# A decoder layer on one core: the first two token blocks are multiplied for v before their norm

## The chip, the cores and the metric

The kernel runs on one core of one Trainium2 chip. The metric is the device time of one execution in microseconds (us), lower is better. The core has five engines with a queue of instructions each: PE (matrix products; loads of the stationary operand are shown as PEld), DVE (elementwise work), ACT (activation functions and copies), POOL (small helpers) and SP (which issues most of the transfers). Each engine works through its own queue in the order in which the instructions stand there, and waits by semaphores for the others.

## The reference, cut to what matters

```python
def layer(x, norm1_g, w_in, ...):                   # x: 512 tokens x 1024 channels
    u = x * rsqrt(mean(x * x, -1) + EPS) * norm1_g  # RMSNorm, one factor for each token
    a_glu, q, k, v, r, g_low, gate_a, gate_b = split(u @ w_in)
    ...                                             # conv branch, gated attention, merge, FFN
```

The change lies in the first few products: `v[:, 0:512] = u @ w_in[:, v columns 0:512]`. It rests on the factor of the norm being one number for each token: `((x * g) @ w) * r` is the same as `(x * g * r) @ w`.

## The kernel before

**Products.** All large products are made of float32 operands split into two parts, a high one in a rounded format (`hi`, made by a copy on ACT) and the remainder (`lo`, made by a subtraction on DVE). A product is three matmuls: low times high, high times low, high times high (`mm3`, L283 to L285). A weight block of 128 x 1024 arrives in a `raw` buffer (three of them) by a DMA that SP issues (L166), and `split_weight` makes `whi` (ACT, L238) and `wlo` (DVE, L241) of it; there are four buffers for each. A list `order` names all weight blocks in the order of use, and `weight()` keeps the splitting two blocks ahead (`LOOK`).

**The first stage.** x is handled in four blocks of 128 tokens (t = 0 to 3). `norm1(t)` squares and sums the block on ACT (L398, with a read of the accumulator), adds EPS on DVE (L400), takes the power -1/2 on POOL (L331) and scales the block on DVE by the factor and the gains (L404, two halves). The gains were spread over all partitions by two matmuls with a row of ones (L389). `to_channels(t)` then turns the block: for each of two groups of four channel tiles, four transposes on PE (L360), a copy to the high part `uh` on ACT (L364) and the subtraction for the low part `ul` on DVE (L365). `u1` holds the result for all later products with `w_in`.

**The products for v.** `values(0, next_tokens)` runs `row_half` with the tokens outside: the four weight blocks of `w_v` are all split first, and then each token block t goes through its eight channel tiles (24 matmuls of 128 x 512) into one PSUM bank. In the middle of a token block (`MID` = 4 tiles) `next_tokens(t)` issues the transposes of block t+1 and `norm1(t+2)`. `v_done` copies each bank out (L428). When the last block is under way, `prefetch` splits the first blocks of the next stage, `w_glu`.

**What sets the order.** Everything up to there stands inside `tc.manual_schedule(engines=START)`: PE, ACT, DVE and SP get their instructions in the order in which the program text issues them. What comes after it (the `w_glu` products, `col_tile`, with the conv taps as filler on DVE) is placed by the planner.

## Time and profile before

| | us |
|---|---|
| median of 3 runs | 855.03 |
| lowest, highest | 854.35, 855.71 |
| the profiled execution's own time | 854.89 |
| its span in the profile | 853.0 |
| PE busy, PEld busy | 839.1, 693.6 |
| DVE busy, ACT busy, POOL busy | 642.9, 373.1, 19.5 |

The profile covers one execution; starts are counted from the start of its span. Rows of instructions read: start, duration, engine, line, operation, output <- inputs, shape, count, and in brackets the idle time of the engine before it with what ended it.

### The profile page before, as it was taken

How to read it: one execution, taken by the hardware profiler on the slowest of the kernel's cores; microseconds unless marked ns; L12 is line 12 of the kernel's file. 1: busy time of each engine (PE TensorE's matmuls, PEld its weight loads, DVE VectorE, ACT ScalarE, POOL GpSimd, SP SyncE). 2: the span in 40 equal slices, each digit the busy share in tenths (PEclk: the TensorE clock that was granted, in tenths of full speed). 3: DMA queues.
4: the chain of work that ended last, by engine and by line, in shares of the span. 5: the costliest groups of instructions: out<-in, count | busy, mean ns of one | idle time of the engine just before them, and what ended most of it. 6: DMA issues, size and time to landing. Idle time of an engine off the chain costs nothing.

```text
span 853.0 us, 9893 instructions
## 1 busy us (share of the span) xinstructions
PE 839.1 (98%) x3838; PEld 693.6 (81%) x3838; DVE 642.9 (75%) x895; ACT 373.1 (44%) x515; POOL 19.5 (2%) x36
## 2 busy tenths in 40 slices
PE   8999999999999999999999999999999999999995
PEld 5888888888888888788888898888888888888884
DVE  5479879999998788744553458779857779857797
ACT  5523337435533522359322336444344445344444
POOL 1000000000100100000000000000000000000001
PEclk9999999999999999999999999999999999999999
DMA  7233232323222332322332163332542222533213
GB/s 274 91 107 107 91 101 88 100 74 99 75 78 80 127 99 99 99 74 90 109 124 102 59 222 124 100 99 75 196 149 98 95 80 75 192 129 100 75 38 111
DMA packets 26848, 91.74 MB, mean 108 GB/s; under 512 B 3041, under 2 KB 3169, under 8 KB 26802
## 3 DMA queue, kind: packets, MB, share of 16 engines
q1 hardware_dynamic: 26802, 91.11, 32.2%
q8 instruction: 30, 0.49, 0.2%
q14 instruction: 16, 0.13, 0.0%
HBM read 89.01 MB, written 2.10 MB: 107 GB/s over the span
## 4 chain that ended last, share of the span: by engine, by line
PE 96%; DVE 2%; DMA 1%; POOL 0%; ACT 0%; issue 0%; SPq 0%; POOLq 0%; DVEq 0%
PE mm L283 30%; PE mm L285 30%; PE mm L284 30%; PE ax L689 1%; DMA raw<-in_w_v_dram 1%; PE ax L360 1%; PE ax L691 1%; PE ax L671 1%; PE ax L283 1%; PE ax L284 1%; PE ax L285 1%; PE ax L658 0%; PE ax L706 0%; PE ax L657 0%; DVE hres L919 0%; DVE wlo L224 0%
## 5 line engine op out<-in xcount | busy, mean ns | idle before, releaser
L283 PE MATMUL mm<-uh,wlo 128*128 128x512 f32 (+1 forms) x768 | 294.8, 384 | 0.0
L285 PE MATMUL mm<-uh,whi 128*128 128x512 f32 (+1 forms) x768 | 292.4, 381 | 0.0
L284 PE MATMUL mm<-ul,whi 128*128 128x512 f32 (+1 forms) x768 | 292.0, 380 | 0.0
L238 ACT CAST whi<-raw 128x1024 fp32r<-128x1024 f32 x124 | 129.5, 1045 | 165.6 <-PE mm L285 134.8
L241 DVE TENSOR_TENSOR wlo<-raw,whi 128x1024 fp32r<-128x1024 f32 x124 | 151.0, 1220 | 52.5 <-ACT whi L238 52.1
L285 PEld LDWEIGHTS mm<-uh,whi 128*128 128x128 f32 x768 | 144.4, 188 | 27.9
L284 PEld LDWEIGHTS mm<-ul,whi 128*128 128x128 f32 x768 | 144.5, 188 | 27.2
L283 PEld LDWEIGHTS mm<-uh,wlo 128*128 128x128 f32 x768 | 144.5, 188 | 27.2
L448 DVE SCALAR_TENSOR_TENSOR c<-h,pp,c 128x511 f32<-128x511 f32 (+14 forms) x240 | 162.6, 732 | 0.7
L828 DVE SCALAR_TENSOR_TENSOR tmp<-mm,pp,tmp 128x511 f32<-128x511 f32 x88 | 65.7, 748 | 60.0 <-ACT tmp L826 58.8
L826 ACT ACTIVATE tmp<-mm,pp 128x512 f32<-128x512 f32 x44 | 34.3, 780 | 70.3 <-PE mm L285 70.3
L223 ACT CAST whi<-kept 128x1024 fp32r<-128x1024 f32 (+1 forms) x24 | 23.3, 975 | 20.7 <-PE mm L285 8.8
L331 POOL TENSOR_TENSOR rstd<-var,mhalf 128x1 f32<-128x1 f32 (+1 forms) x20 | 15.4, 778 | 690.1 <-DVE var L788 473.6
L224 DVE TENSOR_TENSOR wlo<-kept,whi 128x1024 fp32r<-128x1024 f32 (+1 forms) x24 | 26.9, 1129 | 0.5 <-ACT whi L223 0.5
L223 ACT CAST whi<-raw 128x1024 fp32r<-128x1024 f32 (+1 forms) x18 | 17.5, 977 | 21.7 <-PE mm L285 13.8
L283 PE MATMUL mm<-whi,ul 128*128 128x512 f32 x64 | 25.3, 396 | 1.2 <-DVE ul L365 1.2
L285 PE MATMUL mm<-whi,sh 128*128 128x512 f32 x66 | 26.1, 395 | 0.0
L284 PE MATMUL mm<-wlo,sh 128*128 128x512 f32 x66 | 26.1, 395 | 0.0
L283 PE MATMUL mm<-whi,sl 128*128 128x512 f32 x66 | 26.0, 394 | 0.0
L283 PE MATMUL mm<-h,wlo 128*128 128x512 f32 x64 | 25.7, 402 | 0.0
L283 PE MATMUL mm<-whi,h 128*128 128x512 f32 x64 | 25.4, 397 | 0.0
L285 PE MATMUL mm<-h,whi 128*128 128x512 f32 x64 | 25.3, 395 | 0.0
(198 smaller groups left out, 1114.5 us busy)
## 6 DMA issues: line engine op xcount, KB each, us to landing
raw<-in_w_up_dram SPq DMA_DIRECT2D x44, 512.0 KB, 3.4
raw<-in_w_down_dram SPq DMA_DIRECT2D x20, 512.0 KB, 3.4
raw<-in_w_glu_dram SPq DMA_DIRECT2D x16, 512.0 KB, 3.3
kept<-in_w_down_dram SPq DMA_DIRECT2D x10, 512.0 KB, 4.7
raw<-in_w_v_dram SPq DMA_DIRECT2D x8, 512.0 KB, 3.7
raw<-in_w_qk_dram SPq DMA_DIRECT2D x8, 512.0 KB, 3.3
raw<-in_w_r_dram SPq DMA_DIRECT2D x8, 512.0 KB, 3.3
raw<-in_w_gb_dram SPq DMA_DIRECT2D x8, 512.0 KB, 3.3
```

Source lines behind the costliest of these rows:

```text
L223: nc.scalar.copy(hi, raw)
L224: nc.vector.tensor_tensor(lo, raw, hi.bitcast(F32), ALU.subtract)
L238: nc.scalar.copy(hi, raw)
L241: pace[0] = nc.vector.tensor_tensor(lo, raw, hi.bitcast(F32), ALU.subtract)
L283: nc.tensor.matmul(acc, ll, rh, start=first, stop=False, **kw)
L284: nc.tensor.matmul(acc, lh, rl, start=False, stop=False, **kw)
L285: nc.tensor.matmul(acc, lh, rh, start=False, stop=last, **kw)
L331: nc.gpsimd.tensor_tensor(r, v, mhalf[:, :n], ALU.pow)
L360: nc.tensor.transpose(tr[:, k * P : (k + 1) * P], un[:, c : c + P], ident)
L448: nc.vector.scalar_tensor_tensor(y[:, s:], c[:, : T - s], w, y[:, s:], ALU.mult, ALU.add)
L826: nc.scalar.activation(z, acc, AF.Identity, bias=pp[:, PP_FB + m : PP_FB + m + 1], scale=w[2])
L828: nc.vector.scalar_tensor_tensor(z[:, s:], acc[:, : T - s], w[j], z[:, s:], ALU.mult, ALU.add)
```

## The change

Token blocks 0 and 1 (`EARLY` = 2) are no longer normed ahead of the products for the first half of v. Their transposes are multiplied by the gains only (one number for each partition after the transpose; the gains arrive as eight rows by a DMA that ACT issues, and one transpose turns them), split into temporary high and low parts (`eu`), and multiplied with the weights one weight block at a time, both token blocks together (`by_parts`: within a call first all high x high, then weight low x high, then weight high x low). `v_done` scales their banks by the norm's factor `rs[t]`. Their normed form, which all later products need in `u1`, is made later by `normalize(t)`, in the middle of token blocks 2 and 3: a matmul spreads the factors over the partitions, DVE multiplies, ACT makes the high part and DVE the low part. Blocks 2 and 3 (`late_acts`) are scaled ahead of the transpose; the gains are multiplied in behind it. The first two weight blocks are split in halves. `warm(n)` issues n matmuls of ones on PE: 13 at the start, 4 behind the first transposes and one between each two of the first six products; `WARM[2]` and `WARM[3]` are not used. x block 1 is loaded ahead of the second weight block, x block 2 ahead of the constants `pp`. The rest of the program, from the `w_glu` products on, is as before, and stands in the same order on every engine.

```diff
-WARM = 3
+WARM = (13, 4, 2, 3)
 MID = 4
+EARLY = 2
...
             lo = wp.tile([P, D], F32R, tag="wlo", name=nm("wlo"), bufs=4)
+            if halves:
...
+                cols = [slice(j * T, (j + 1) * T) for j in range(2)]
+                for c in cols:
+                    nc.scalar.copy(hi[:, c], raw[:, c])
+                return [lambda c=c: low(c) for c in cols]
...
+    nc.scalar.dma_start(rows8, a["norm1_g"].rearrange("(k p) -> k p", p=P))
     load_x(0)
-    load()
     load()
     load_x(1)
     load()
-    gain1 = [mm_bank(), mm_bank()]
-    for j in range(2):
-        nc.tensor.matmul(gain1[j], ones[0:1, :], row[:, j * T : (j + 1) * T], start=True, stop=True)
...
+    load()
+    load_x(2)
+    warm(WARM[0])
+    nc.tensor.transpose(idle[:, P : P + KT], rows8, ident[0:KT, 0:KT])
+    nc.vector.tensor_copy(gains, idle[:, P : P + KT])
...
+    def with_gain(tr, g):
+        f = heap()
+        by_channel = gains[:, g * 4 : g * 4 + 4].unsqueeze(2).to_broadcast([P, 4, P])
+        nc.vector.tensor_tensor(by_four(f), by_four(tr), by_channel, ALU.mult)
+        return f
...
+    def normalize(t):
+        r = ax_bank()
+        nc.tensor.matmul(r[:, :P], rs[t].to_broadcast([P, P]), ident, start=True, stop=True)
+        for g in range(2):
+            f = by_four(xg[t, g])
+            nc.vector.tensor_tensor(f, f, r[:, :P].unsqueeze(1).to_broadcast([P, 4, P]), ALU.mult)
+            hi, lo = in_u1(t, g)
+            high(hi, f)
+            low(lo, f, hi)
+
+    def late_acts(t):
+        nc.vector.tensor_scalar(xs[t], xs[t], rs[t], None, ALU.mult)
+        for g in range(2):
+            f = by_four(with_gain(transposed(xs[t], g), g))
+            hi, lo = in_u1(t, g)
+            high(hi, f)
+            low(lo, f, hi)
...
-        nc.scalar.copy(vt[t, n], acc)
+        if n == 0 and t < EARLY:
+            nc.scalar.activation(vt[t, n], acc, AF.Copy, scale=rs[t])
+        else:
+            nc.scalar.copy(vt[t, n], acc)
...
-    values(0, next_tokens)
+    early_acts(0, 0)
+    early_high(0, 0)
+    early_acts(0, 1)
+    warm(WARM[1])
+    lows = split_weight(True)
+    lows[0]()
+    early_low(0, 0)
+    lows[1]()
+    load()
+    early_high(0, 1)
+    early_low(0, 1)
+    accs = [mm_bank() for _ in range(EARLY)]
+    by_parts(accs[0], 0, (0, 1), lambda: warm(1))
+    squares(0)
+    early_acts(1, 0)
+    early_high(1, 0)
+    early_low(1, 0)
+    early_acts(1, 1)
+    by_parts(accs[1], 1, (0, 1))
+    for part in split_weight(True):
+        part()
+    load_x(3)
+    load()
+    early_high(1, 1)
+    early_low(1, 1)
+    squares(1)
+    for t in range(EARLY):
+        by_parts(accs[t], t, (2, 3))
+    split_weight()
+    for t in range(EARLY):
+        by_parts(accs[t], t, (4, 5))
+    squares(2)
+    late_acts(2)
+    split_weight()
+    for t in range(EARLY):
+        by_parts(accs[t], t, (6, 7))
+        v_done(t, 0, accs[t])
+    for t in range(EARLY, NT):
+        acc = mm_bank()
+        by_parts(acc, t, range(4))
+        if t == EARLY:
+            squares(3)
+            late_acts(3)
+        normalize(t - EARLY)
+        by_parts(acc, t, range(4, KT))
+        if t == NT - 1:
+            prefetch(LOOK)
+        v_done(t, 0, acc)
```

More of the change, by code (lines that the diff above doesn't have):

```diff
@@ L211, in sum_down, with split_weight @@
         return raw
-    def split_weight(between=None):
+    def split_weight(halves=False, between=None):
         if len(ready) < len(order):
@@ L237, in split_weight, with low @@
             lo = wp.tile([P, D], F32R, tag="wlo", name=nm("wlo"), bufs=4)
+            if halves:
+                ready.append((hi, lo))
+                def low(c):
+                    nc.vector.tensor_tensor(lo[:, c], raw[:, c], hi[:, c].bitcast(F32), ALU.subtract)
+                cols = [slice(j * T, (j + 1) * T) for j in range(2)]
+                for c in cols:
+                    nc.scalar.copy(hi[:, c], raw[:, c])
+                return [lambda c=c: low(c) for c in cols]
             nc.scalar.copy(hi, raw)
-            if between:
-                between()
             pace[0] = nc.vector.tensor_tensor(lo, raw, hi.bitcast(F32), ALU.subtract)
@@ L368, in trunk_layer @@
     u1 = new_acts()
-    row = tp.tile([P, D], F32, tag="gain", name=nm("row"), bufs=1)[0:1, :]
+    acts1 = by_k(u1)
     nc.vector.memset(ones, 1.0)
     nc.gpsimd.memset(mhalf, -0.5)
-    xs = {}
+    xs, rs, xg, eu = {}, {}, {}, {}
     def load_x(t):
@@ L376, in load_x, with by_four @@
         nc.sync.dma_start(xs[t], a["x"][t * P : (t + 1) * P, :])
+    def by_four(t):
+        return t.rearrange("p (k t) -> p k t", k=4)
     start = tc.manual_schedule(engines=START)
     start.__enter__()
-    nc.sync.dma_start(row, a["norm1_g"].unsqueeze(0))
+    rows8 = tp.tile([P, P], F32, tag="gain", name=nm("gains"), bufs=1)[0:KT, :]
+    nc.scalar.dma_start(rows8, a["norm1_g"].rearrange("(k p) -> k p", p=P))
     load_x(0)
-    load()
     load()
@@ L385, in trunk_layer, with warm @@
     load()
-    gain1 = [mm_bank(), mm_bank()]
-    for j in range(2):
-        nc.tensor.matmul(gain1[j], ones[0:1, :], row[:, j * T : (j + 1) * T], start=True, stop=True)
-    warm = ax_bank()
-    for _ in range(WARM):
-        nc.tensor.matmul(warm[:, :P], ident, ident, start=True, stop=True)
-    def norm1(t):
-        xt = xs[t]
+    load()
+    load_x(2)
+    idle = ax_bank()
+    def warm(n):
+        for _ in range(n):
+            nc.tensor.matmul(idle[:, :P], ones, ones, start=True, stop=True)
@@ new lines, in trunk_layer, with transposed @@
+    gains = cp.tile([P, KT], F32, name="gains")
+    warm(WARM[0])
+    nc.tensor.transpose(idle[:, P : P + KT], rows8, ident[0:KT, 0:KT])
+    nc.vector.tensor_copy(gains, idle[:, P : P + KT])
+    def transposed(x, g):
+        tr = ax_bank()
+        for k in range(4):
+            c = (g * 4 + k) * P
+            nc.tensor.transpose(tr[:, k * P : (k + 1) * P], x[:, c : c + P], ident)
+        return tr
+    def with_gain(tr, g):
[3 more added lines that the diff above has]
+        return f
@@ L397, in norm1, with in_u1, high, low @@
+    def in_u1(t, g):
+        return [x[:, :, t * P : (t + 1) * P] for x in u1[g]]
+    def high(hi, f):
+        nc.scalar.copy(hi, f)
+    def low(lo, f, hi):
+        nc.vector.tensor_tensor(lo, f, hi.bitcast(F32), ALU.subtract)
+    def squares(t):
         ss = small(1, "ss")
-        nc.scalar.activation(junk(D), xt, AF.Square, scale=1.0 / 32.0, accum_out=ss)
+        nc.scalar.activation(junk(D), xs[t], AF.Square, scale=1.0 / 32.0, accum_out=ss)
         v = small(1, "var")
         nc.vector.tensor_scalar(v, ss, EPS, None, ALU.add)
-        r = rsqrt(v, 1)
@@ L402, in norm1 @@
-        for j in range(2):
-            s = slice(j * T, (j + 1) * T)
-            nc.vector.scalar_tensor_tensor(xt[:, s], xt[:, s], r, gain1[j], ALU.mult, ALU.mult)
-    norm1(0)
-    split_weight()
-    split_weight(lambda: to_channels(xs[0], u1, 0, (0,)))
-    to_channels(xs[0], u1, 0, (1,))
-    load_x(2)
-    norm1(1)
-    split_weight()
-    split_weight()
-    load_x(3)
-    acts1 = by_k(u1)
-    def next_tokens(t):
-        if t + 1 < NT:
-            to_channels(xs[t + 1], u1, t + 1)
-        if t + 2 < NT:
-            norm1(t + 2)
+        rs[t] = tp.tile([P, 1], F32, tag="r1", name=nm("r1"), bufs=NT)
@@ new lines, in squares, with early_acts, early_high, early_low @@
+        nc.gpsimd.tensor_tensor(rs[t], v, mhalf[:, :1], ALU.pow)
+    def early_acts(t, g):
+        xg[t, g] = with_gain(transposed(xs[t], g), g)
+        eu[t, g] = [by_four(heap(F32R)) for _ in range(2)]
+    def early_high(t, g):
+        high(eu[t, g][0], by_four(xg[t, g]))
+    def early_low(t, g):
+        low(eu[t, g][1], by_four(xg[t, g]), eu[t, g][0])
+    def normalize(t):
[7 more added lines that the diff above has]
+            low(lo, f, hi)
@@ L427, in v_done, with by_parts @@
         vt[t, n] = heap()
-        nc.scalar.copy(vt[t, n], acc)
-    def values(n, middle):
-        row_half("w_v", n * KT // 2, n, acts1, KT, v_done, n == 1, middle)
-    values(0, next_tokens)
+        if n == 0 and t < EARLY:
+            nc.scalar.activation(vt[t, n], acc, AF.Copy, scale=rs[t])
+        else:
+            nc.scalar.copy(vt[t, n], acc)
+    ws = [order[j] for j in range(KT // 2)]
+    assert ws == [("w_v", j) for j in range(KT // 2)]
+    used[0] = len(ws)
+    def by_parts(acc, t, ks, between=None):
+        for i, (wi, ai) in enumerate(((0, 0), (1, 0), (0, 1))):
+            for k in ks:
+                act = eu[t, k // 4][ai][:, k % 4, :] if t < EARLY else acts1[k][ai][:, t * P : (t + 1) * P]
+                j = slice((k % 2) * T, (k % 2 + 1) * T)
+                first, last = k == 0 and i == 0, k == KT - 1 and i == 2
+                nc.tensor.matmul(acc, act, ready[k // 2][wi][:, j], start=first, stop=last)
+                if between:
+                    between()
+    early_acts(0, 0)
[46 more added lines that the diff above has]
+        v_done(t, 0, acc)
     start.__exit__(None, None, None)
@@ L581, in gate @@
                 nc.vector.tensor_tensor(ls[h], ls[h], ab[h], ALU.subtract)
-    values(1, gate)
+    row_half("w_v", KT // 2, 1, acts1, KT, v_done, True, gate)
     def gl(n, tag, bufs):
```

## The prediction, made before the changed kernel ran

> **What bounds the kernel now.** I read the page first, then the waits of PE, then the timeline of the first 40 us.

> ```profile
> span 853.0 us, 9893 instructions
> PE 839.1 (98%) x3838; PEld 693.6 (81%) x3838; DVE 642.9 (75%) x895; ACT 373.1 (44%) x515; POOL 19.5 (2%) x36
> ...
> PE mm L389 <- DMA row<-in_norm_g_dram: 2.4, 1, 2.4
> PE mm L283 <- DVE ul L365: 1.2, 1, 1.2
> PE mm L283 <- DVE hres L919: 0.8, 1, 0.8
> ```

> The reader is to see that PE is the bound: the third-longest wait of PE in 853 us is already 0.8 us, so what delays PE in the first stage delays the end one for one, and what lets it start sooner can be won. The timeline shows how the first stage runs (start, duration, engine, line).

> ```profile
> 0.90 0.17 DVE L370 MEMSET ones<- 128x128 f32 x1 [0.90 <-PEq L1063]
> 2.45 3.75 PE L389 MATMUL mm<-row,ones 1*128 1x512 f32 x4 [2.45 <-DMA row<-in_norm_g_dram]
> 4.52 1.06 ACT L398 ACTIVATE junk<-x 128x1024 bf16<-128x1024 f32 x1 [2.44 <-DMA x<-in_x_dram]
> 6.12 1.65 PE L393 MATMUL ax<-ident 128*128 128x128 f32 x6
> 7.57 1.82 PE L360 MATMUL ax<-ident,x 128*128 128x128 f32 x8
> 10.62 0.50 PE L283 MATMUL mm<-whi,ul 128*128 128x512 f32 x1 [1.24 <-DVE ul L365]
> ...
> 20.11 0.39 PE L285 MATMUL mm<-whi,uh 128*128 128x512 f32 x1
> 20.79 0.40 PE L285 MATMUL mm<-whi,uh 128*128 128x512 f32 x1
> 21.02 1.04 PE L360 MATMUL ax<-ident,x 128*128 128x128 f32 x8
> 36.47 0.39 PE L283 MATMUL mm<-uh,wlo 128*128 128x512 f32 x1
> ```

> The first product for v starts at 10.62, the first of `w_glu` at 36.47. A warm product takes 0.227 us of PE (three in 20.79 - 20.11 = 0.68). Eight transposes take 1.04 us warm and 1.82 cold: 0.11 and 0.21 each. Between 10.62 and 36.47 lie 25.85 us: 96 products (21.8) and 24 transposes (2.7), with 1.4 us of waits. The change rebuilds only this stretch; from the first product of `w_glu` on the order is the old one. So the sum is the new start of that product against 36.47, added to the profiled execution's own 854.89 us (the median of the runs, 855.03, is 0.14 more).

> **The prices.** Groups of the first 40 us, then of the whole run, then single rows of the timeline and of the chain.

> ```profile
> L241 DVE TENSOR_TENSOR wlo<-raw,whi 128x1024 fp32r<-128x1024 f32 x8 | 9.7, 1221 | 5.7 <-ACT whi L238 5.4
> L238 ACT CAST whi<-raw 128x1024 fp32r<-128x1024 f32 x8 | 8.4, 1050 | 4.6 <-DMA raw<-in_w_v_dram 2.2 <-PE mm L285 1.4 <-DMA raw<-in_w_glu_dram 1.0
> L404 DVE SCALAR_TENSOR_TENSOR x<-x,rstd,mm 128x512 f32<-128x512 f32 x8 | 5.6, 745 | 2.8 <-POOL rstd L331 2.8
> L365 DVE TENSOR_TENSOR ul<-ax,uh 128x512 fp32r<-128x512 f32 x8 | 5.2, 686 | 4.7 <-ACT uh L364 4.7
> L398 ACT ACTIVATE junk<-x 128x1024 bf16<-128x1024 f32 x4 | 4.2, 1060 | 4.0 <-DMA x<-in_x_dram 4.0
> L428 ACT COPY h<-mm 128x512 f32<-128x512 f32 x4 | 2.4, 589 | 3.3 <-PE mm L285 3.3
> L331 POOL TENSOR_TENSOR rstd<-var,mhalf 128x1 f32<-128x1 f32 x4 | 2.2, 554 | 19.8 <-DVE var L400 19.8
> L398 ACT ACTIVATION_READ_ACCUMULATOR junk<-x 128x1 f32 x4 | 0.8, 190 | 0.0
> L400 DVE TENSOR_SCALAR var<-ss 128x1 f32<-128x1 f32 x4 | 0.6, 152 | 5.7 <-ACT junk L398 5.5
> ...
> L525 ACT CAST h<-h 128x512 fp32r<-128x512 f32 x8 | 5.0, 625 | 3.0 <-DVE h L771 3.0
> ...
> 32.59 1.05 ACT L238 CAST whi<-raw 128x1024 fp32r<-128x1024 f32 x1 [0.77 <-PE mm L285]
> 33.68 3.94 DVE L241 TENSOR_TENSOR wlo<-raw,whi 128x1024 fp32r<-128x1024 f32 x3 [3.74 <-ACT whi L238]
> 842.84 0.49 DVE L892 TENSOR_SCALAR hres<-hres,rstd 128x512 f32<-128x512 f32 x1 [0.44 <-POOL rstd L331]
> 844.33 1.19 DVE hres L919 x2
> ```

> A pass of DVE over 128x512 takes 0.69 until the next engine may go on, and 0.60 until DVE's next one (two in 1.19). ACT's copy to the high part takes 0.62 from SBUF. A hand-over from engine to engine is 0.04 (33.68 after 32.59 + 1.05).

> **What decides: pairs in turn.** The new forms of the activations cost DVE two passes for each group of four channel tiles, where it had one besides the norm: `with_gain` or the multiplication in `normalize` makes f, ACT makes the high part of f, DVE the low part. On DVE's queue the order is f, low, f, low: low waits for ACT, and the next f stands behind low. So a group costs 0.69 + 0.04 + 0.62 + 0.04 + 0.60 = 2.0 us in turn, of which DVE works 1.3. Blocks 2, 3, 0 and 1 have two groups each: 16 us of such pairs, in a stage in which PE has 12 us of products for blocks 2 and 3.

> **The start of the products.** Removed are the gain matmuls, the wait for their row, and the chain squares, EPS, POOL, scaling ahead of the first transposes. x block 0 is issued first (it was second), so it lands some 0.4 us before 4.5. But 13 warm-up matmuls now stand ahead of its transposes: as L393 shows, one float32 matmul is two records (six for `WARM` = 3), so they are 26, and from 1.1 us (ones set at 0.90 + 0.17) at 0.21 each they last to 6.7. The trace has one case of PE's speeding up: eight slow transposes up to 9.39, fast products from 10.62, so 7 to 8 us after its first work at 2.45. With the same here it comes at 8 or 9, and all 26 are slow. Then: transposes of the first group 6.9 to 7.9, f 8.6, high part 9.25, half of the first weight block on ACT 9.8. First product at 9.8, 0.8 sooner than before. If PE speeds up after 3.5 us, it is 8.4.

> **To the second weight block.** Six products with six warm-ups between them (0.22 each, fast by then) and 0.6 of waits for the halves of `wlo` end at 13.1; block 1's transposes, f and high part come in turn (0.44 + 0.2 + 0.69 + 0.62 + hand-overs), and token block 1's products start at 15.2 after 1.1 of waiting. ACT meanwhile has in its queue: the high part, two halves of the second weight block, the other high part, squares(1) with its read (1.06 + 0.19), and only then the third weight block: 18.2 to 19.2, its `wlo` 20.5. PE's 12 products with it end at 22.8.

> **The first new stall.** Behind them stand the transposes of block 2 on PE, and on ACT both its high parts ahead of the fourth weight block's. The chain is one transposed group (0.6), f, high, low, f, high (0.69 + 0.62 + 0.60 + 0.69 + 0.53), `whi` (1.05) and six hand-overs: 5.0 us, of which PE works 0.9 on transposes. It stands for 4.1 us, and after two products for 0.8 more, until `wlo` of that block is there (1.22 behind `whi`). It goes on at 27.8, and blocks 0 and 1 are done at 31.35.

> **The second new stall.** ACT now copies out the two banks, 0.59 each, and only then squares block 3, though that has long landed: copy 0.6, squares 1.25, EPS 0.15, POOL 0.55, scaling by one number over 128x1024, transposes 0.6. No row has that scaling; it lies between 0.49 (L892, half the size) and 1.22 (a two-operand pass of that size), I take 0.8, near the first, of the same operation. With hand-overs the first f of block 3 starts at 35.65. From there six pairs (block 3, then `normalize(0)` and `normalize(1)`) at 2.0 are 12.0, and behind them stand the first blocks of `w_glu` on the same two queues: `whi` 1.05 and `wlo` 1.22, of which 0.6 lies beside the last low part. That is 49.2. PE from 31.35 has 48 products (10.9), eight transposes (0.9), two small matmuls (0.4) and 0.9 of waiting for block 3: done at 44.5, and waits 4.8 us for `wlo`, which its first `w_glu` product reads.

> **The sum.** 49.2 - 36.47 = 12.7 us. As a check by terms: start 0.8 sooner; warm-ups between products and factor matmuls +1.8; early waits +2.5; stalls 4.1 + 0.8 + 0.9 + 4.8 = 10.6; the old waits of 1.4 gone: 12.7. So 854.89 + 12.7 = 867.6.

> **What costs nothing.**

> ```profile
> raw<-in_w_v_dram SPq DMA_DIRECT2D x8, 512.0 KB, 3.7
> x<-in_x_dram SPq DMA_DIRECT2D x4, 512.0 KB, 5.3
> ```

> On SP the fourth weight block waits until `wlo`'s second half of the first is made (11.7) and lands 3.7 later, 15.4; ACT takes it at 26.7. Block 3 of x is behind it and lands by 17.5 to 21, needed at 32. The `w_glu` blocks follow by 22, needed at 46. Should these covers go, each would only lengthen a chain that is later anyway. The gains' DMA on ACT stands before any work of ACT. POOL's four powers wait in turn as before. The scale in `v_done` rides on a copy that was there.

> **Bounds.** The clock's start: 47.8 to 49.3. The passes with gains at 0.745 (as L404) for 0.69, eight of them in the chains: +0.5. The scaling: -0.3 to +0.4. Hand-overs of 0.06 for 0.04: +0.5. So 866 to 869 for this case.

> [...]

> ```profile
> 844.35 0.40 PE L285 MATMUL mm<-whi,ah 128*128 128x512 f32 x1
> ...
> 844.80:848.80 4.00, 0.00 (x0) 0.00 (x0) 2.83 (x8) 2.44 (x6) 1.42 (x2) 1.00 0.56 207
> 848.90:853.00 4.10, 0.00 (x0) 0.00 (x0) 0.11 (x1) 0.35 (x1) 0.00 (x0) 0.50 0.68 251
> ```

> At the end PE idles from 844.75, and the granted clock (third column from the right) is 1.00 for four more microseconds, then 0.50. So an idle stretch of about 4 us can halve it, and both stalls are that long. If it happens, products take about twice as long (as the transposes did at the start, 0.21 for 0.11) until PE has been busy again for a while, 7 to 8 us there as an upper end; with 3 to 6 us that is 1.5 to 3 us for each stall, 869 to 873. [...] The trace agrees with a delay of about 4 us.

> **The rivals.** (a) The forecast: 867.6, chance 0.64. (b) Forecast plus the halved clock: about 870. The stalls are just at the length that the one case of the trace shows: chance 0.18. (c) The pairs overlap on DVE: a group then costs DVE's own work, 1.3 for 2.0. The second chain shortens by 4.2 us, the first by at most 0.7: about 863. Against it stands the order of the queue; for it, that DVE is free a third of the time. Chance 0.11. (d) The other side: PE bounds the stage, since all pairs hide. Then the early start counts: 9.8 + 26.2 of PE work = 36.0, or 34.6 with the early clock: 853.0 to 854.4. This decides once the second chain fits PE's 12.2 us: 4.3 + 6p + 1.6 below 12.2, p below 1.05; DVE's own two passes are 1.3, so only a chain that starts sooner as well would do. Chance 0.04. Another 0.03 goes to what I have not thought of. That the change should not do what it says I see no way for: the four queues are written out in program order.

> **How the numbers follow.** A measurement of this kernel can tell about 0.2% (1.7 us) from no change. Faster by more: half of (d) and a little, 0.03; within: the other half, 0.02; slower: 0.95. The range leaves out the ends of (b) and (c): 862.5 to 872.

> **What would show it.** Right: in the profile after, PE's longest waits are of about 4 us for `whi` or `wlo` in the first 50 us, DVE's rows alternate f and low with ACT's copy between, and the first `w_glu` product starts near 49. Wrong: f of the next group starts before low of this one; or that product starts before 40 us.

## The result, and the profile after

| | before | after |
|---|---|---|
| median of the runs (us) | 854.7 (854.35 to 855.71, 4 runs) | 866.67 (866.02 to 867.43, 4 runs) |
| profiled execution (us) | 854.89 | 866.07 |
| its span (us) | 853.0 | 864.0 |
| first product for `w_glu` starts (us) | 36.47 | 51.22 |

The ratio after to before is 1.0137, with an interval of 1.0123 to 1.0151: the change costs 1.4%. The forecast was 867.6, in a range of 862.5 to 872.0. The span and the row of busy times of the page after:

```profile
span 864.0 us, 9987 instructions
PE 842.2 (97%) x3879; PEld 701.3 (81%) x3879; DVE 648.9 (75%) x908; ACT 375.2 (43%) x521; POOL 19.5 (2%) x36
```

PE's busy time rose by 3.1 us, the span by 11.0: most of the loss is idle time of PE. The waits of PE (line, what it waits for: us in total, times, longest) say where:

```profile
PE mm L293 <- DVE wlo L251: 4.4, 1, 4.4
PE mm L496 <- ACT whi L250: 3.9, 1, 3.9
PE ax L408 <- DVE ones L382: 1.1, 1, 1.1
PE mm L496 <- ACT h L433: 1.0, 1, 1.0
```

The first two rows are waits that before did not have. The timeline of after (start, duration, engine, line) shows both with what goes on beside them:

```profile
1.11 5.76 PE L408 MATMUL ax<-ones 128*128 128x128 f32 x26 [1.11 <-DVE ones L382]
9.57 0.50 PE L496 MATMUL mm<-whi,h 128*128 128x512 f32 x1 [0.62 <-ACT whi L248]
22.65 1.04 PE L420 MATMUL ax<-ident,x 128*128 128x128 f32 x8
27.60 1.22 PE L496 MATMUL mm<-whi,h 128*128 128x512 f32 x2 [3.92 <-ACT whi L250]
33.59 0.69 ACT L481 ACTIVATE h<-mm,r 128x512 f32<-128x512 f32 x1 [1.87 <-PE mm L496]
36.17 0.75 DVE L468 TENSOR_SCALAR x<-x,r 128x1024 f32<-128x1024 f32 x1 [0.66 <-POOL r L444]
37.73 0.69 DVE L426 TENSOR_TENSOR h<-ax,gains 128x512 f32<-128x512 f32 x1 [0.81 <-PE ax L420]
45.65 0.68 DVE L462 TENSOR_TENSOR h<-h,ax 128x512 f32<-128x512 f32 x1
46.37 0.62 ACT L433 CAST uh<-h 128x512 fp32r<-128x512 f32 x1 [0.87 <-DVE h L462]
47.02 0.69 DVE L436 TENSOR_TENSOR ul<-h,uh 128x512 fp32r<-128x512 f32 x1 [0.69 <-ACT uh L433]
47.63 0.68 DVE L462 TENSOR_TENSOR h<-h,ax 128x512 f32<-128x512 f32 x1
48.34 0.62 ACT L433 CAST uh<-h 128x512 fp32r<-128x512 f32 x1 [1.36 <-DVE h L462]
49.94 2.36 DVE L251 TENSOR_TENSOR wlo<-raw,whi 128x1024 fp32r<-128x1024 f32 x2 [0.25 <-ACT whi L250]
51.22 0.80 PE L293 MATMUL mm<-uh,wlo 128*128 128x512 f32 x1 [4.41 <-DVE wlo L251]
```

Read DVE from 45.65 on: f (L462), then ACT's high part (L433), then the low part (L436), and only then the next f, 1.98 us after the last one. The `w_glu` weights (L251) stand behind all of them, and PE stands still for 4.41 us.

What the waits alone don't show is in the windows of after (stretch, length, busy time and count of PE, PEld, DVE, ACT, POOL, then the granted clock, DMA share, GB/s):

```profile
23.70:27.00 3.30, 0.00 (x0) 0.00 (x0) 1.93 (x4) 1.63 (x3) 0.00 (x0) 1.00 0.00 1
27.10:33.80 6.70, 6.16 (x14) 4.42 (x15) 1.45 (x2) 1.34 (x3) 0.00 (x0) 0.50 0.26 78
33.90:46.80 12.90, 12.32 (x60) 9.74 (x58) 6.76 (x11) 4.82 (x9) 0.55 (x1) 1.00 0.00 0
46.90:50.90 4.00, 0.00 (x0) 0.00 (x0) 2.94 (x4) 2.64 (x5) 0.00 (x0) 1.00 0.00 0
51.00:54.30 3.30, 3.08 (x7) 2.51 (x8) 2.53 (x3) 1.28 (x2) 0.00 (x0) 0.50 0.60 187
54.40:58.00 3.60, 3.60 (x17) 2.99 (x16) 1.23 (x1) 2.33 (x2) 0.00 (x0) 1.00 0.94 270
```

Behind each stall the granted clock is 0.50: for 6.8 us behind the first, for 3.4 behind the second. From start to start a product takes 0.43 us there (behind the second stall they start at 51.81, 52.24 and 52.67), about twice the 0.227 of full pace.

The third part of the account lies far from the change. A product deep in the kernel can be followed by its own start: the shift, its start after minus its start before, is 14.75 us at the first `w_glu` product, 16.31 seven products later, 16.07 at 292 us, and from there it falls, in stretches and without a jump, to 13.5 at 494, 11.7 at 753, 11.2 at 841. PE has no wait in that stretch, in either kernel. Windows from one product to the same product, 480.95 to 741.05 of before and 494.46 to 752.78 of after:

```profile
480.95:741.05 260.10, 260.10 (x1246) 218.24 (x1245) 198.93 (x256) 116.46 (x147) 1.66 (x3) 1.00 0.36 118
...
494.46:752.78 258.32, 258.31 (x1246) 218.00 (x1245) 198.10 (x255) 116.51 (x147) 1.65 (x3) 1.00 0.35 119
```

The same 1246 products, PE busy throughout, the clock full in both, and 1.78 us less. So the account of the 11.0 us is: stage up to `w_glu` +14.75, half clock behind it +1.56, quicker products later -5.1, the last few us -0.2.

### The profile page after: what moved, and what is told of

Same layout as the page of the kernel before. It is cut to its first block, busy times and chain, and to the rows that moved or that the text cites. A ratio compares the mean times of both kernels' runs of the same rounds, so it can differ in the third digit from the quotient of the medians.

```text
span 864.0 us, 9987 instructions
## 1 busy us (share of the span) xinstructions
PE 842.2 (97%) x3879; PEld 701.3 (81%) x3879; DVE 648.9 (75%) x908; ACT 375.2 (43%) x521; POOL 19.5 (2%) x36
## 4 chain that ended last, share of the span: by engine, by line
PE 94%; DVE 3%; ACT 1%; issue 0%; POOL 0%; POOLq 0%; ACTq 0%
PE mm L293 29%; PE mm L295 28%; PE mm L294 28%; PE mm L496 1%; PE ax L803 1%; PE ax L408 1%; PE ax L785 1%; PE ax L805 1%; PE ax L293 1%; PE ax L294 1%; PE ax L295 1%; DVE h L426 1%; ACT uh L433 1%; DVE ul L436 0%; PE ax L370 0%; PE ax L772 0%
## 5 line engine op out<-in xcount | busy, mean ns | idle before, releaser
L250 ACT CAST whi<-raw 128x1024 fp32r<-128x1024 f32 x122 | 127.3, 1045 | 160.3 <-PE mm L295 128.2
L251 DVE TENSOR_TENSOR wlo<-raw,whi 128x1024 fp32r<-128x1024 f32 x122 | 148.6, 1220 | 48.4 <-ACT whi L250 48.4
L341 POOL TENSOR_TENSOR rstd<-var,mhalf 128x2 f32<-128x2 f32 (+1 forms) x16 | 13.3, 837 | 666.3 <-DVE var L902 469.9
L225 ACT CAST whi<-raw 128x1024 fp32r<-128x1024 f32 (+1 forms) x18 | 17.5, 978 | 21.9 <-PE mm L295 13.2
L293 PE MATMUL mm<-ch,wlo 128*128 128x512 f32 x64 | 25.1, 393 | 0.0
L295 PE MATMUL mm<-ch,whi 128*128 128x512 f32 x64 | 25.0, 391 | 0.0
## 6 DMA issues: line engine op xcount, KB each, us to landing
raw<-in_w_up_dram SPq DMA_DIRECT2D x44, 512.0 KB, 3.4
raw<-in_w_down_dram SPq DMA_DIRECT2D x20, 512.0 KB, 3.4
raw<-in_w_glu_dram SPq DMA_DIRECT2D x16, 512.0 KB, 3.4
kept<-in_w_down_dram SPq DMA_DIRECT2D x10, 512.0 KB, 4.3
raw<-in_w_v_dram SPq DMA_DIRECT2D x8, 512.0 KB, 3.5
raw<-in_w_qk_dram SPq DMA_DIRECT2D x8, 512.0 KB, 3.3
raw<-in_w_r_dram SPq DMA_DIRECT2D x8, 512.0 KB, 3.4
raw<-in_w_gb_dram SPq DMA_DIRECT2D x8, 512.0 KB, 3.3
```

Source lines behind the costliest of these rows:

```text
L225: nc.scalar.copy(hi, raw)
L250: nc.scalar.copy(hi, raw)
L251: pace[0] = nc.vector.tensor_tensor(lo, raw, hi.bitcast(F32), ALU.subtract)
L293: nc.tensor.matmul(acc, ll, rh, start=first, stop=False, **kw)
L295: nc.tensor.matmul(acc, lh, rh, start=False, stop=last, **kw)
L341: nc.gpsimd.tensor_tensor(r, v, mhalf[:, :n], ALU.pow)
```

## The experiments

After this result the theory had two parts. **Theory P**: pairs in turn make the two stalls, and the stalls bring the half clock, at about 2.0 us before `w_glu` and 1.6 after. **Theory A**: the quicker products have nothing to do with the order of the work. The change adds a 32-byte tile (`gains`) and a set of small ones (`r1`) ahead of tiles allocated later. How far that moves them is the author's reckoning from the order and the sizes of the tiles in the two programs; no trace shows an address, and all offsets below are of this reckoning. By it weights and `uh`/`ul` move by 32 bytes per partition, and the heap, the convolution's and the FFN's tiles (the heap family below) by 160; modulo 256 bytes the two families (weights, then heap) stood at 64 and 192 before, and stand at 96 and 96 after; `gains` moves both families alike, and it is the set `r1`, allocated between them, that changes the distance of the heap from the weights, from 128 to 0. The rival to A was that the later start itself, against DMA and the other engines, makes the products quicker.

### Before, with the later tiles moved by 128 bytes

An unused tile is all that is added; the heap family then stands at 64, as the weights do.

```
     ps = pool("psum", 1, bass.MemoryType.PSUM)
+    pool("pad", 1).tile([P, 32], F32, name="pad")
     heap_scope, hp = scoped("heap", 26)
```

> The kernel before with one change: an unused tile of 128 bytes per partition in front of the heap, so that the heap, the conv and the FFN tiles lie 128 bytes higher. Nothing else moves. Theory A (addresses): a product whose operands come from the heap or the FFN tiles takes 0.232 us before and 0.227 after because these tiles lie at another offset modulo 256 bytes than the weight buffers (192 against 64 before, 96 and 96 after); with the pad they lie at 64 and 64, so some 1,000 products win 0.005 us each: about 849.5 us, 5 less than before. Theory B (the faster products after come from the shifted schedule or from chance of the run): 854.7, no change.

Measured: 851.15 us (850.79 to 851.93) beside 856.52 for the kernel before on that chip, ratio 0.9934 (0.9919 to 0.9948), with the first `w_glu` product at 36.72 as before. The shift against before falls, in stretches, to -4.1 at 829 us, and the sequence of instructions is that of before on PE, DVE, ACT and POOL. This is Theory A, shown with the order of before. It also beats both kernels.

### After, with the same tile

The same line in the changed kernel takes its heap family to 224, away from the weights' 96.

> The changed kernel with the same unused tile of 128 bytes in front of the heap: the heap and the FFN tiles now lie at 224 modulo 256 and the weights at 96. Theory A (addresses): the 0.005 us of each such product come back, about 872 us, 5 more than after, and the change is worth +17 against a kernel before of the same layout. Theory B: 866.7, no change.

Measured: 871.3 us (870.88 to 872.09), ratio to before 1.0169 (1.0153 to 1.0184). The stalls are those of after, 3.9 and 4.4 us, but behind the second one the half clock lasted twice as long in this execution, 6.8 us for 3.4. So the shift against after goes from -0.56 at the first `w_glu` product to 0.76 at 56 us by the clock; the rest of it, to 3.3 at 484 us and 6.1 at 850, is the pace of the products, 5.3 us. Groups by form (last number before the bar's end: mean ns of one) of before, of after, of before with the tile and of after with it:

```profile
L283 PE MATMUL mm<-whi,sl 128*128 128x512 f32 x66 | 26.0, 394 | 0.0
L283 PE MATMUL mm<-h,wlo 128*128 128x512 f32 x64 | 25.7, 402 | 0.0
```

```profile
L293 PE MATMUL mm<-whi,sl 128*128 128x512 f32 x66 | 25.7, 390 | 0.0
L293 PE MATMUL mm<-h,wlo 128*128 128x512 f32 x64 | 25.4, 397 | 0.0
```

```profile
L284 PE MATMUL mm<-whi,sl 128*128 128x512 f32 x66 | 25.7, 390 | 0.0
L284 PE MATMUL mm<-h,wlo 128*128 128x512 f32 x64 | 25.4, 397 | 0.0
```

```profile
L294 PE MATMUL mm<-whi,sl 128*128 128x512 f32 x66 | 26.0, 394 | 0.0
L294 PE MATMUL mm<-h,wlo 128*128 128x512 f32 x64 | 25.7, 402 | 0.0
```

394 and 402 ns go with 64/192 and 96/224, a distance of 128, and 390 and 397 with 96/96 and 64/64, a distance of 0, whichever kernel it is: in these groups the placement moves the pace, the order does not. (A matmul's duration in these rows overlaps the next one's; from start to start it is 0.232 against 0.227 us: twelve products of `sl` and `sh` take 2.79 us in before, 588.51 to 591.30, and 2.72 in after, 601.80 to 604.52.) The rival, the later start, falls: after and after with the tile start `w_glu` within 0.6 us of each other (51.22 and 50.66) and have different paces.

### Before, with 64, 256 and 384 bytes

Three more kernels, each run once, ask which offsets matter. The edit is the same line with `[P, 16]`, `[P, 64]` and `[P, 96]`.

> The kernel before with 64 bytes in front of the heap: heap tiles at 0 modulo 256, weight buffers at 64. Theory A1 (what counts is that the offsets of the two operands agree modulo 256): slow as before, products of the heap near 0.232 us, about 855. Theory A2 (the old place of the heap was a bad one, any other is good): near 0.227, about 850.

> The kernel before with 256 bytes in front of the heap: heap tiles at 192 modulo 256 again, weight buffers at 64. Theory A1 (offsets modulo 256): exactly as before, 0.232 us, about 855. Theory A2 (any other place is good): 0.227, about 850. A rule modulo 512 that wanted another distance would also differ from the run with 128.

> The kernel before with 384 bytes in front of the heap: heap tiles at 64 modulo 256, as the weight buffers, but 256 bytes from the place that the run with 128 gave them. Theory A1 (modulo 256): fast, 0.227 us, about 850. Rival (modulo 512, or the one place): 0.232, about 855.

Measured: 256 bytes, which leaves all offsets modulo 256 as they were, 856.12 us, with before's paces (394 and 402 ns) and one wait of 1.0 us at 200 us that before does not have; 384 bytes, the offsets of 128, 852.06 with 390 and 397, of which 1.5 us is a half clock at 836.5 that the run with 128 does not have. So 256 bytes of room change nothing (855.84 for before beside 856.12), and the effect of 128 comes again with 256 more. 64 bytes takes the heap family to 0, and lies between, 853.46:

```profile
L284 PE MATMUL mm<-whi,sl 128*128 128x512 f32 x66 | 25.8, 391 | 0.0
...
L284 PE MATMUL mm<-h,wlo 128*128 128x512 f32 x64 | 25.7, 402 | 0.0
```

One group is quick and the other slow, 391 and 402 ns, and even the products of `sh` differ there, 389 ns with `whi` and 394 with `wlo`, though both weights come from the same family. "The offsets must be equal" is therefore not the whole rule; which difference of which operands costs the 0.005 us stays open.

### After, with PE kept busy in the two stalls

Matmuls of `ones` on a spare bank fill the stalls and change nothing else in the order.

```
     late_acts(2)
+    fill_up(14)
     split_weight()
...
             prefetch(LOOK)
+            fill_up(16)
```

> The changed kernel with matmuls of ones on PE in its two long stalls: 14 behind the transposes of token block 2 (3.0 us of the 3.9 us stall), 16 behind the last product of token block 3 (3.4 us of 4.4). They shorten no chain. Theory A (the idle stretch halves the clock): no half clock at 27 and at 51 us, the 22 products after the first stall end 2.4 us sooner, the second chain starts that much sooner, and the products of w_glu run at full pace at once, 1.7 us more: about 862.5. Theory B (the slow products lie beside the chains of DVE and ACT and cost nothing): 866.7; and fillers that came in the way would make it slower, 867 to 869.

Measured: 862.86 us (862.48 to 863.37), ratio to before 1.0069 (1.0054 to 1.0084). Windows of this kernel over the first stall, the products behind it, and the tail:

```profile
23.00:27.00 4.00, 3.21 (x29) 3.02 (x28) 2.38 (x5) 2.18 (x3) 0.00 (x0) 1.00 0.00 0
27.00:33.00 6.00, 5.47 (x24) 4.19 (x24) 1.20 (x2) 2.41 (x4) 0.25 (x1) 1.00 0.26 87
...
848.10:851.40 3.30, 3.30 (x9) 2.60 (x8) 2.86 (x8) 2.06 (x4) 1.49 (x2) 0.50 0.12 45
```

The real work waits as long as it did, but the clock behind it is 1.00. The first `w_glu` product starts at 48.39, 2.83 us sooner than in after: 0.76 of that is there from the first product on (8.81 for 9.57, since the clock rose at 4.98 us in this execution and at 6.59 in that of after), the other 2.1 is the half clock's. Seven products later the gain is 4.26, so 1.4 for the second stall. That is Theory P's price for the clock, shown: 2.1 and 1.4 us for 2.0 and 1.6. The last row is a half clock near the end, which after did not have in that place; there the gain shrinks from 4.30 to 2.73 us.

### After, with both f ahead of both pairs

```
 def normalize(t):
-    for g in range(2):
-        f = by_four(xg[t, g])
+    fs = [by_four(xg[t, g]) for g in range(2)]
+    for f in fs:
         nc.vector.tensor_tensor(f, f, ..., ALU.mult)
+    for g, f in enumerate(fs):
         hi, lo = in_u1(t, g)
```

and the same in `late_acts`.

> The changed kernel with another order on DVE in late_acts and normalize: both f of a token block first, then the two high parts and the two low parts, so that DVE no longer waits for ACT inside a group. Theory A (pairs in turn decide both stalls): the first chain loses 1.3 us, the second 3 x 1.5 = 4.5; both idle stretches become shorter than 3 us, so the clock stays full, another 4: about 857. Theory B (something else holds the weights back: the splitting of the weights on ACT, or their DMA): within 1 us of 866.7.

Measured: 859.81 us (858.94 to 860.4), ratio 1.0037 (1.0025 to 1.005), slower than the 857 that was expected. Its timeline on DVE and PE, then its windows:

```profile
38.45 1.29 DVE L436 TENSOR_TENSOR ul<-h,uh 128x512 fp32r<-128x512 f32 x2
40.85 1.28 DVE L462 TENSOR_TENSOR h<-h,ax 128x512 f32<-128x512 f32 x2 [1.11 <-PE ax L459]
42.23 1.29 DVE L436 TENSOR_TENSOR ul<-h,uh 128x512 fp32r<-128x512 f32 x2
45.06 0.50 PE L293 MATMUL mm<-uh,wlo 128*128 128x512 f32 x1 [1.47 <-DVE wlo L251]
```

```profile
22.00:25.40 3.40, 0.91 (x9) 0.68 (x7) 2.58 (x4) 2.16 (x3) 0.00 (x0) 1.00 0.03 11
25.45:28.80 3.35, 3.31 (x7) 2.20 (x8) 1.21 (x1) 0.00 (x0) 0.00 (x0) 0.50 0.34 108
844.65:848.00 3.35, 3.35 (x10) 2.57 (x9) 2.91 (x8) 2.06 (x4) 1.49 (x2) 0.50 0.11 42
```

Two f now stand next to each other, then two low parts: 2.7 us for two groups (40.85 to 42.23 + 1.29 = 43.52) where the old order took 4.0. Ahead of the last two DVE now waits 1.11 us for PE, so the second chain loses less than its three pairs save. `w_glu` starts 6.17 us sooner than in after: 0.79 from the earlier first product, 1.4 from the first stall (2.54 for 3.92), 2.9 from the second (1.47 for 4.41); the 1.1 that is left goes with a half clock of 3.4 us for 6.8. This is Theory P's other half, shown. The miss against 857 is the clock: a stall of 2.5 us, thought too short, halved it too, and so did the tail, which gave back 1.5 of the 7.6 us.

### After, with the chains started sooner as well

On top of the last edit the scaling of x is taken out of `late_acts`, the fourth weight block goes ahead of block 2's pairs, and block 3's squares and scaling ahead of the copies of v:

```
     squares(2)
-    late_acts(2)
+    scaled(2)
     split_weight()
+    late_acts(2)
+    squares(3)
     for t in range(EARLY):
         by_parts(accs[t], t, (6, 7))
         v_done(t, 0, accs[t])
+    scaled(3)
...
-            squares(3)
```

> The changed kernel with three steps of order: both f of a group pair first (as in the run with pairs), the fourth weight block split before token block 2's high and low parts, and the squares and the scaling of token block 3 before the copies of blocks 0 and 1. The same work, nothing left out. Theory A (the stalls are queue order on ACT and DVE, and the half clock follows from them): no stall at the fourth weight block, no half clock at 27 us, about half a microsecond of stall ahead of w_glu; its first product starts near 42 instead of 51, the end at 866.7 - 9.4 - 1.7 = 855.6, a ratio to before of 1.001. Theory B (the work added on DVE and ACT bounds the stage whatever its order): the first product of w_glu stays beyond 45, the end near 860 or later.

Measured: 853.92 us (852.39 to 855.36) beside 855.84 for before (12 runs), ratio 0.9975 (0.9964 to 0.9987); `w_glu` starts at 39.54, 2.5 us sooner than was expected. The timeline of PE:

```profile
22.77 0.71 PE L499 MATMUL mm<-whi,h 128*128 128x512 f32 x2
...
39.54 0.50 PE L293 MATMUL mm<-uh,wlo 128*128 128x512 f32 x1 [1.48 <-DVE wlo L251]
```

The first stall is gone, the second is 1.48 us long (half a microsecond was expected), and no half clock follows it. This is faster than before, but only by the placement it has from the change: its `w_glu` still starts 3.1 us later than before's (39.54 to 36.47), and before with 128 bytes, which stands nearly as well placed (its later products win 4.3 us by the shift, those of after 5.1), is at 0.9934. On that footing the rebuilt first stage costs about 0.4% in its best order here (0.9975 / 0.9934 = 1.004) and 2.0% in the order of the change (1.0137 / 0.9934 = 1.020).

## Why the number held, and which steps did not

The forecast's time held, 866.67 for 867.6, but partly by two errors of 3.6 and 5.1 us that cancel, and that they do is luck. Step by step:

| step of the prediction | predicted (us) | measured (us) |
|---|---|---|
| **the start of the products** | 9.8 | 9.57 |
| block 2's transposes, behind 12 products of the third weight block | 22.8 | 22.65 |
| **the first new stall** | 4.1, goes on at 27.8; 0.8 more after two products | 3.92, at 27.60; 0.04 of PE after two products, which ran at half clock until 28.8 |
| first f of block 3 (**the second new stall**) | 35.65 | 37.73 |
| from there to the first `w_glu` product | 13.55 | 13.49 |
| length of that stall | 4.8 | 4.41 |
| first `w_glu` product | 49.2 | 51.22 |
| shift that remains at the end (**the sum**) | 12.7 | 11.0 in the span |

**Pairs in turn** was right, and to the tenth: 1.98 us from f to f for 2.0, and the six pairs with the `wlo` behind them 13.49 for 13.55. The experiment with both f first shows that it was the queue's order, not DVE's work: the same passes take 2.7 us for two groups. Both signs named as wrong (f of the next group ahead of this one's low part, and `w_glu` before 40) did not come. The scaling, priced at 0.8 between two bounds, took 0.75.

**The clock** is where the forecast's own case was wrong. Rival (b) had a chance of 0.18, and it came, in both stalls. It was sized rightly, 1.5 to 3 us each for 2.0 and 1.6 here; the chance was too low. The step that failed is the reading that "an idle stretch of about 4 us can halve it" and that the stalls are "just at the length that the one case of the trace shows": one end of the trace showed that 4 us were enough, and it was read as if less were not. The runs show all stalls of 2.5 us and over followed by the half clock: 3.9 and 4.4 in after, 3.9 and 4.4 with the tile, 2.5 with both f first; those of 1.5 (with both f first, and with the chains started sooner) were not. With the clock the sum should have been 867.6 + 3.6 = 871.2. The 3 to 6 us of slow products in (b), and the 3.5 us of an early clock at the start, were the author's assumptions, which no run of before shows: after has half clocks of 6.8 and 3.4 us, and full clock 5.5 us after PE's first matmul (1.11 to 6.59), with the stalls filled 3.9 (1.12 to 4.98).

**The sum** failed in its premise that from the first `w_glu` product on "the order is the old one" and so the time too. The order was; the pace of its products was not. That gave 5.1 us back, 871.2 - 5.1 = 866.1, the 866.07 of the profiled execution. No rival held this: nothing in the prediction looked at where the added tiles push the others. Taken by itself, the reordering costs more than the comparison shows: 1.7% if the kernel keeps a placement as slow as before's (1.0169 with the tile), 2.0% if both stand well.

Rivals (c) and (d) did not come with this change; (c) is what the edit with both f first does, and it shows the price put on it, 4.2 us in the second chain and up to 0.7 in the first, near in the sum and wrong in its parts: 2.9 and 1.4 less stall.

## What to carry to other kernels

When two engines hand a tile back and forth (f, high part, low part), issue all first steps of a batch ahead of all last ones: the pair in turn cost 1.98 us for each group here, with both f first two groups took 2.7, and everything behind the pairs, here the next stage's weights, was late (a stall of 4.41 us against one of 1.47). A stall of PE of 2.5 us or more had a second price here beside its length, products at half clock behind it, 2.0 and 1.6 us in after; filling both stalls with idle matmuls bought 2.1 and 1.4 back. And 128 unused bytes in front of the heap moved the kernel before to 0.9934 of its time and the changed one from 1.0137 of before's to 1.0169: compare two kernels with the same placement before the order is praised or blamed for the last half per cent.

## What the runs showed of the hardware

```profile
844.70:848.00 3.30, 1.74 (x7) 0.94 (x6) 3.30 (x6) 2.19 (x4) 0.00 (x0) 1.00 0.00 0
```

  How much work keeps the clock is not settled: 3.21 of 4.00 us did in the filled stall. PE's busy time alone does not order the cases. In before with 384 bytes a stretch with 1.83 us of it was followed by the half clock (first row; the 22 products of `wlo` and `ah` into `mm`, the last of which lie behind it, took 420 ns in the mean for 394 with 128 bytes); in before with 128 bytes one with 1.55, all at its start, was followed by a stretch at full clock (second and third row):

```profile
833.10:836.50 3.40, 1.83 (x7) 1.03 (x6) 3.40 (x5) 2.19 (x4) 0.00 (x0) 1.00 0.00 0
...
839.00:842.40 3.40, 1.55 (x7) 0.94 (x5) 3.40 (x8) 2.53 (x6) 0.43 (x2) 1.00 0.69 255
842.45:845.80 3.35, 0.00 (x0) 0.00 (x0) 1.29 (x4) 1.45 (x2) 1.21 (x2) 1.00 0.45 168
```

- **The pace of full-speed products changed with unused bytes ahead of the heap.** In the kernel before the products of `sl` with `whi` took 394 ns without such bytes (855.84 us) and with 256 (856.12 us), 391 with 64 (853.46 us), and 390 with 384 (852.06 us) and 128 (851.15 us, where before took 856.52); in the changed kernel 390 became 394 with 128 (871.3 us). From start to start that is 0.227 or 0.232 us, worth some 5 us in 855. Products of `uh` with `whi`, both allocated ahead of those bytes, show no such step (390 ns in before and after, 390 and 391 in them with 128 bytes). Not every group follows: `ch` with `whi` took 391 ns in before and after and 395 in both with 128 bytes. By the reckoned offsets only two remainders of the heap's distance from the weights were tried more than once, 128 (slow) and 0 (quick). Why, and by which operand, was not separated.
